# New tokens' scores in a two-layer hybrid decoder step: split products against plain fp32 products

## The chip, the cores and the metric

The kernel runs on one core of one Trainium2 chip. The metric is the device time of one execution in microseconds. Three runs of the kernel before are shown; one more execution was recorded by the hardware profiler, and all rows below come from that one.

## What is computed

Two layers of a decoder run over 1,024 prompt tokens and 64 new tokens (8 sequences of 8). Each layer projects its input to nine parts, mixes one branch with a spatial gMLP (layer norm, a 128x128 product per channel group), mixes the other with three dilated windows of causal attention, gates and merges both, and adds the result. The change touches the scores of the new tokens in window group 0 against the cached keys, and in all three groups against the new keys:

```python
def dilated_gather_attention(q, k_all, v_all, dil, n_back):
    ...
    kg = jnp.take(k_all, idx, axis=1)
    vg = jnp.take(v_all, idx, axis=1)
    s = jnp.einsum('bthd,btjhd->bhtj', q, kg,
                   preferred_element_type=jnp.float32) * (HEAD_DIM ** -0.5)
    s = jnp.where(valid[None, None], s, NEG)
    lse = jax.nn.logsumexp(s, axis=-1)
    p = jnp.exp(s - lse[..., None])
    ...
def att_sample(q, k, v, layer=l):
    ...
    k_all = jnp.concatenate([buf[:, :, 0], k[:, :, g]], axis=1)
```

All data are fp32. Group 0 has 128 cached keys per sequence, all read; the cached keys of groups 1 and 2 are scored elsewhere, on GpSimd and VectorE.

## The kernel before

**The projections set the order.** Per layer 80 jobs (`JOBS`, one job for 128 output columns) are each cut into three pieces of 384, 384 and 320 tokens. A piece (`piece`, L733) is 24 matmuls: weight and activation are each held as a high and a low part in fp32r, and a product is three matmuls (L741). After the third and the sixth of the eight contraction blocks, and behind the piece, `tick` is called. When no attention of the prompt is under way, each tick runs one step of the background queue `bgq` (`bg_step`, L434): first `sample` (L1167), then, in layer 0, `ada` (L555), which prepares the modulation of this layer's end and of the next layer. What a step emits thus stands on TensorE between two thirds of a piece, in an order fixed when the program is written; TensorE runs it in that order and waits where an operand is late.

**The spatial gMLP** (`gmlp`, L1050) sits in a second queue, `urgent`, from the end of the v jobs on. `bg_step` reaches it only when `bgq` is empty; `sample` lets it run where it calls `hurry` (L484), which is also the start of `idle` (L492); `pause` (L488) only gives up steps. The first u job (`ev_u`, L1156) needs it finished: `drain` (L473) then runs the background alone, without pieces between. At the end of a layer another drain (L1603) empties all queues.

**The scores of the new tokens** (`weights` in `sample`, L1204) take two sequences at a time (rg 0 to 3). For each sequence its queries are copied into a block layout `big` and split into high and low parts, twelve small operations on ScalarE and VectorE (L1212, L1213); the new keys are split too (L1214); the cached keys come split from `half_stream` (L315). Then 8 matmuls score the cached keys (L1223) and 24 matmuls of 8 columns the new ones (L1231), and the two halves are added from PSUM (L1236, L1237). Softmax (L1259 to L1263), transposes (L1268) and `outputs` (L1285: value products L1299 to L1311, a reduction on VectorE L1317, a matmul L1321 that waits for it) follow. `units` (L1188) gives the order: scores 0 and 1, outputs 0, scores 2, outputs 1, scores 3, outputs 2 and 3.

Of the kernel before, what the change touches and what calls it, by code (L numbers as in the profile page):

```python
# [32 lines left out]
NB = 8  # L33
# [3 lines left out]
L = 2  # L37
# [142 lines left out]
class Builder:  # L180
# [326 lines left out]
    def setup(self):  # L507
# [28 lines left out]
        self.s_d = [[d([8, NB, NT, 128], f"sd{l}{g}") for g in (1, 2)] for l in range(L)]  # L536
        self.vn_d = [d([3, SMP, 512], f"vnd{l}") for l in range(L)]
# [629 lines left out]
    def sample(self, l):  # L1167
        nc, a, ident = self.nc, self.a, self.pk("ident")
        whole = self.apool.tile([128, 6144], FR, name=self.nm("qb"), tag="act")
        big = whole[:, 0:768]  # L1170
        pt = whole[:, 768:1536].rearrange("p (a b) -> p a b", b=128)
        qs, kn = [whole[:, o:o + 768].bitcast(FT).rearrange("p (a b) -> p a b", b=SMP) for o in (1536, 2304)]
        vw = whole[0:24, 3072:4096].rearrange("p (a b) -> p a b", a=2)
        sel2 = whole[:, 4096:4160]
        knh = whole[:, 4160:4352].rearrange("p (a b c) -> p a b c", a=2, b=12)
        for t, d in ((qs, self.qs_d[l]), (kn, self.kn_d[l])):
            self.load(t, d.rearrange("c p t -> p c t"))
        t = self.half(name="sel2")[:, 0:64]
        self.load(t, a["pack"][:, NPACK:NPACK + 64])
        nc.gpsimd.memset(whole[:, 0:768].bitcast(FT), 0.0)  # L1180
        nc.vector.memset(whole[:, 768:1536].bitcast(FT), 0.0)
        pstep = list(big.ap[0])[0]

        def diag(off, ap, h2):
            v = big[64 * h2:64 * h2 + 64]
            return bass.AP(tensor=v.tensor, offset=v.offset + off, ap=[[pstep, 64]] + ap)
# [3 lines left out]
        for x, rg in units:  # L1190
            for b in (2 * rg, 2 * rg + 1):
                if x == "v":
                    seq += [a["vc1"][l, b, i] for i in range(2)]
                seq.append(a[x + "c0"][l, b])
# [6 lines left out]
        yield from self.idle(2)  # L1201
        pn = {}

        def weights(rg):  # L1204
            rows = self.slot([128, 1024], name="rows")[:, 0:408]
            for b2 in range(2):
                b = 2 * rg + b2
                cols = slice(8 * b, 8 * b + 8)
# [7 lines left out]
                s = [self.ps("s") for _ in range(2)]  # L1216
                hi, lo = next(st)
                for kt in range(4):
                    first, last = kt % 2 == 0, kt % 2 == 1
                    c = slice(kt * 128, kt * 128 + 128)  # L1220
                    mm = [(64, hi), (32, lo)]
                    for m, t in (mm[::-1] if last else mm):
                        nc.tensor.matmul(s[kt // 2][0:m, 0:128], big[:, kt * 64:kt * 64 + m], t[:, c],  # L1223
                                         start=first and m == 64, stop=last and m == 64)
                yield
                for g in range(3):
                    for kt in range(4):
                        base = g * 256 + kt * 64
                        mm = [(64, 0), (32, 1)]
                        for m, e in (mm[::-1] if kt % 2 else mm):  # L1230
                            nc.tensor.matmul(s[kt // 2][0:m, 128 + 8 * g:136 + 8 * g], big[:, base:base + m],  # L1231
                                             knh[:, e, g * 4 + kt, :], start=kt % 2 == 0 and m == 64,
                                             stop=kt % 2 == 1 and m == 64)
                for qd in range(2):
                    t = self.half(name="slo")[0:32, 0:152]
                    self.copy(t, s[qd][32:64, 0:152])  # L1236
                    nc.vector.tensor_tensor(rows[64 * b2 + 32 * qd:64 * b2 + 32 * qd + 32, 128:280], s[qd][0:32, 0:152], t,  # L1237
                                            op=OP.add)
                yield
                yield from self.hurry()  # L1240
# [4 lines left out]
            def scores_in():  # L1245
                for b2 in range(2):
                    for g, o in ((1, 0), (2, 280)):
                        d = self.s_d[l][g - 1]
                        self.load(rows[64 * b2:64 * b2 + 64, o:o + 128],
                                  bass.AP(tensor=d.tensor, offset=d.offset + 1024 * (2 * rg + b2),  # L1250
                                          ap=[[8192, 8], [128, 8], [1, 128]]))
                went.append(True)
# [4 lines left out]
            yield from self.idle(3)  # L1257
# [7 lines left out]
            yield from self.idle(4)  # L1265
# [72 lines left out]

    def q_places(self, qs, pr, cols, h2):
        out = []  # L1340
        for g in range(3):
            src = qs[pr, 4 * g:4 * g + 4, cols].rearrange("p (a b) t -> p a b t", b=2)
            out.append((256 * g + 8 * h2, [[128, 2], [80, 2], [1, 8]], src))
# [361 lines left out]
```

## Time and profile before

| what | value |
|---|---|
| three runs | 3125.6, 3126.67 and 3132.71 us, median 3126.67 us |
| the profiled execution, its time | 3128.81 us |
| its span, first to last instruction | 3127.0 us |
| mean granted TensorE clock | 0.983 of full speed |
| TensorE busy | 3001.5 us, 96% of the span, 19136 matmul records |
| VectorE, GpSimd, ScalarE busy | 54%, 44% and 39% of the span |

In the views below a row of a timeline is one instruction or a merged run of one kind, with its start and duration in us. Matmuls are pipelined, so durations overlap; the time that a group takes is read from its start to the start of the next row. A bracket is the idle time before the row and what ended it. An fp32 matmul leaves two records in the trace, a transpose or an fp32r matmul one.

### The profile page before, as it was taken

How to read it: one execution, taken by the hardware profiler on the slowest of the kernel's cores; microseconds unless marked ns; L12 is line 12 of the kernel's file. 1: busy time of each engine (PE TensorE's matmuls, PEld its weight loads, DVE VectorE, ACT ScalarE, POOL GpSimd, SP SyncE). 2: the span in 40 equal slices, each digit the busy share in tenths (PEclk: the TensorE clock that was granted, in tenths of full speed). 3: DMA queues.
4: the chain of work that ended last, by engine and by line, in shares of the span. 5: the costliest groups of instructions: out<-in, count | busy, mean ns of one | idle time of the engine just before them, and what ended most of it. 6: DMA issues, size and time to landing. Idle time of an engine off the chain costs nothing.

```text
span 3127.0 us, 51203 instructions
## 1 busy us (share of the span) xinstructions
PE 3001.5 (96%) x19136; PEld 2860.7 (91%) x19136; DVE 1702.8 (54%) x3583; ACT 1230.0 (39%) x3085; POOL 1363.7 (44%) x959
## 2 busy tenths in 40 slices
PE   6998999999999999999999989999999999999998
PEld 4998899989999998879989988999999899999998
DVE  7444545463266656466773555464632757553666
ACT  5454444444233133343434544444442331322433
POOL 4665547463144223123446655564731542322343
PEclk8999999999999999999999999999999999999999
DMA  6335243434354334466544253434344542434665
GB/s 223 117 100 113 97 88 119 94 107 95 111 189 142 105 119 163 162 239 228 194 161 130 91 121 99 88 123 85 119 88 128 176 150 89 137 103 144 220 214 178
DMA packets 251537, 425.93 MB, mean 136 GB/s; under 512 B 103852, under 2 KB 158392, under 8 KB 251288
## 3 DMA queue, kind: packets, MB, share of 16 engines
q1 hardware_dynamic: 251288, 422.65, 44.7%
q8 instruction: 151, 2.47, 0.3%
q14 instruction: 98, 0.80, 0.1%
HBM read 349.96 MB, written 72.61 MB: 135 GB/s over the span
## 4 chain that ended last, share of the span: by engine, by line
PE 82%; DVE 7%; DMA 4%; issue 2%; ACT 2%; POOL 1%; SPq 0%; DVEq 0%; ACTq 0%; POOLq 0%
PE pspj L741 53%; PE pspj L1377 13%; PE pss L870 4%; PE pso L916 3%; PE pspt L895 2%; DMA kq<-in_kc_dram 1%; DMA craw<-in_wada_dram 1%; PE psmi L602 1%; DVE chl L249 1%; PE psmi L993 1%; PE pspt L1310 1%; DVE act L249 1%; PE pspt L1127 1%; PE pso L1127 1%; PE pss L1094 1%
## 5 line engine op out<-in xcount | busy, mean ns | idle before, releaser
L741 PE MATMUL pspj<-act,whi 128*128 128x384 f32 (+1 forms) x7680 | 1965.8, 339 | 6.2 <-DVE act L674 3.7
L741 PEld LDWEIGHTS pspj<-act,whi 128*128 128x128 f32 x7680 | 1350.9, 190 | 42.1 <-issue 6.6
L741 PE MATMUL pspj<-act,wlo 128*128 128x384 f32 (+1 forms) x3840 | 1263.0, 329 | 2.3 <-POOL wlo L247 2.3
L249 POOL TENSOR_TENSOR wlo<-wraw,whi 128x1024 fp32r<-128x1024 f32 x154 | 373.2, 2424 | 906.0 <-ACT whi L243 764.4
L741 PEld LDWEIGHTS pspj<-act,wlo 128*128 128x128 f32 x3840 | 728.2, 190 | 3.4 <-POOL wlo L247 3.4
L1377 PE MATMUL pspj<-act,whi 128*128 128x384 f32 (+1 forms) x1536 | 373.5, 326 | 0.5 <-ACT act L243 0.4
L243 ACT ACTIVATE whi<-wraw 128x1024 fp32r<-128x1024 f32 x280 | 294.0, 1052 | 124.3 <-DMA wraw<-in_wgm_dram 49.4
L247 POOL TENSOR_TENSOR wlo<-wraw,whi 128x512 fp32r<-128x512 f32 x126 | 192.2, 1532 | 325.5 <-ACT whi L243 274.7
L882 ACT ACTIVATE ssb<-ssb,ast 128x128 f32<-128x128 f32 (+1 forms) x384 | 170.2, 444 | 380.4 <-DVE ast L878 380.4
L878 DVE CUSTOM_DVE_ANT_0 ssb<-pss,pack 128x128 f32<-128x128 f32 (+1 forms) x384 | 119.4, 348 | 326.7 <-PE pss L870 325.7
L1377 PEld LDWEIGHTS pspj<-act,whi 128*128 128x128 f32 x1536 | 270.2, 188 | 1.0 <-ACT act L243 0.7
L1377 PE MATMUL pspj<-act,wlo 128*128 128x384 f32 (+1 forms) x768 | 250.3, 326 | 0.3 <-POOL wlo L247 0.3
L1005 ACT ACTIVATE th<-pspj 128x384 f32<-128x384 f32 x168 | 79.2, 471 | 422.3 <-PE pspj L741 375.9
L787 POOL TENSOR_TENSOR r<-r,sin 128x384 f32<-128x384 f32 x144 | 139.1, 966 | 175.7 <-DVE r L786 169.9
L249 DVE TENSOR_TENSOR chl<-craw,chl 128x512 fp32r<-128x512 f32 x182 | 155.4, 882 | 86.8 <-ACT chl L243 85.1
L377 POOL TENSOR_TENSOR kq<-kq,qb 128x1024 f32<-128x1024 f32 x64 | 152.6, 2390 | 66.5 <-DMA kq<-in_kc_dram 32.0
L381 POOL TENSOR_TENSOR kq<-kq,qb 128x512 f32<-128x512 f32 x128 | 167.3, 1312 | 30.3 <-DMA kq<-in_kc_dram 25.3
L386 DVE TENSOR_REDUCE sc<-kq 128x16 f32<-128x1024 f32 x128 | 155.7, 1217 | 13.0 <-POOL kq L377 12.9
L870 PE MATMUL pss<-kz,q 128*128 128x256 f32 x560 | 156.2, 387 | 5.6 <-ACT kz L240 5.6
L430 POOL TENSOR_TENSOR vq<-vq,pv 128x1024 f32<-128x1024 f32 x64 | 134.8, 2115 | 49.2 <-DMA vq<-in_vc_dram 25.9
L1377 PEld LDWEIGHTS pspj<-act,wlo 128*128 128x128 f32 x768 | 144.2, 188 | 0.6 <-POOL wlo L247 0.6
L247 DVE TENSOR_TENSOR wlo<-wraw,whi 128x512 fp32r<-128x512 f32 x126 | 108.0, 858 | 43.7 <-ACT whi L243 40.7
(211 smaller groups left out, 3676.6 us busy)
## 6 DMA issues: line engine op xcount, KB each, us to landing
wraw<-in_win_dram SPq DMA_DIRECT2D x160, 512.0 KB
kq<-in_kc_dram SPq DMA_DIRECT2D x64, 512.0 KB
vq<-in_vc_dram SPq DMA_DIRECT2D x64, 512.0 KB
craw<-in_wada_dram SPq DMA_DIRECT2D x48, 512.0 KB
wraw<-in_wgm_dram SPq DMA_DIRECT2D x48, 512.0 KB
wraw<-in_wo_dram SPq DMA_DIRECT2D x48, 512.0 KB
kq<-in_kc_dram SPq DMA_DIRECT2D x64, 256.0 KB
craw<-in_vc_dram SPq DMA_DIRECT2D x32, 512.0 KB
```

The lines of the kernel that those rows point to most:

```text
L243: self.nc.scalar.activation(hi, src, AF.Copy)
L247: e.tensor_tensor(lo[:, c], src[:, c], hi[:, c].bitcast(FT), op=OP.subtract)
L249: (eng or self.nc.vector).tensor_tensor(lo, src, hi.bitcast(FT), op=OP.subtract)
L377: nc.gpsimd.tensor_tensor(v, v, x, op=OP.mult)
L381: nc.gpsimd.tensor_tensor(v[:, f], v[:, 1], x[f], op=OP.mult)
L386: nc.vector.tensor_reduce(sc[:, :, i].rearrange("p h j -> p j h"), ts.pop(i)[0].rearrange("p a (j h d) -> p (a j) h d", h=2, d=64), axis=A ...
L430: nc.gpsimd.tensor_tensor(v, v, p.unsqueeze(3).to_broadcast([128, 2, 8, 64]), op=OP.mult)
L741: nc.tensor.matmul(ps[:, :w], a[:, k, :], h[:, b, k, :w], start=(n == 0), stop=(n == 23))
L787: nc.gpsimd.tensor_tensor(t2, t2, self.sin[:, s], op=OP.mult)
L870: nc.tensor.matmul(s[:, 256 * j:256 * j + 256], u["q"][:, 128 * b:128 * b + 128], self.kz[:, (b - n + j) % 4].rearrange("p h c -> p (h c)" ...
L882: nc.scalar.activation(x[:, h, :w], x[:, h, :w], AF.Exp, bias=st[:, h * 8 + b:h * 8 + b + 1], scale=-1.0, accum_out=st[:, 16 + h * 8 + b:1 ...
L1377: self.nc.tensor.matmul(ps[:, :w], ws[a][:, k, :], hs[b][k][:, :w], start=(n == 0), stop=(n == 3 * nk - 1))
```

## The change

The queries of all sequences are placed once in a block layout `qd` in plain fp32, by DMA into a zeroed tile. All new keys are scored at the start for all sequences in 12 fp32 matmuls of 64 columns (L1209), which give every sequence against every sequence; the result goes through DRAM (`n_d`), and each pair of sequences reads its own 24 columns back. For the cached keys a pair is one batch: its queries are copied into `kz`, the zeroed tile of the prompt's attention, as eight 128x128 blocks, and 8 fp32 matmuls (L1234) add into one PSUM tile. The raw keys are loaded at the start of the pair instead of coming split from the stream. Some `idle` calls become `pause`, and `hurry` stands once at the start of `weights`. The shortened diff:

```diff
+        qd = whole[:, 1536:3072].bitcast(FT).rearrange("p (a b) -> p a b", b=2 * SMP)
...
+        nc.gpsimd.memset(whole[:, 1536:3072].bitcast(FT), 0.0)
+        nc.gpsimd.memset(kz, 0.0)
+        self.load(kn, self.kn_d[l].rearrange("c p t -> p c t"))
+        for h2 in range(2):
+            r = slice(64 * h2, 64 * h2 + 64)
+            self.load(qd[r, :, r], self.qs_d[l][:, r].rearrange("c p t -> p c t"))
...
+        def keys_in(rg):
+            raws[rg] = self.slot([128, 2, 512], name="kraw")
+            for b2 in range(2):
+                self.load(raws[rg][:, b2], a["kc0"][l, 2 * rg + b2])
...
+        t = self.slot([128, 4, 192], name="sn")
+        for g0, n in ((0, 2), (2, 1)):
+            ps = self.ps("s")
+            for c in range(4 * n):
+                nc.tensor.matmul(ps[:, 64 * c:64 * c + 64], qd[:, 4 * g0 + c], kn[:, 4 * g0 + c], start=True, stop=True)
+            for g in range(n):
+                self.copy(t.rearrange("p k (b g t) -> p (k b) g t", b=8, g=3)[:, :, g0 + g],
+                          ps[:, 256 * g:256 * g + 256].rearrange("p (k t) -> p k t", t=8))
+            yield
+        self.store(self.n_d[l].rearrange("k p x -> p k x"), t)
...
         def weights(rg):
+            yield from self.hurry()
             rows = self.slot([128, 1024], name="rows")[:, 0:408]
+            keys_in(rg)
+            for h2 in range(2):
+                v = kz[64 * h2:64 * h2 + 64]
...
+            yield from self.pause(4)
+            k = raws.pop(rg)
+            s = self.ps("s")
             for b2 in range(2):
-                for h2 in range(2):
-                    for o, ap, src in self.q_places(qs, slice(64 * h2, 64 * h2 + 64), cols, h2):
-                        hi, lo = diag(o, ap, h2), diag(o + 32, ap, h2)
-                        self.copy(hi, src)
-                        nc.vector.tensor_tensor(lo, src, hi.bitcast(FT), op=OP.subtract)
-                self.split(knh[:, 0], knh[:, 1], kn[:, :, cols])
-                yield from self.idle(2)
...
                 for kt in range(4):
+                    i = 4 * b2 + kt
+                    nc.tensor.matmul(s[:, 0:128], kz[:, 128 * i:128 * i + 128], k[:, b2, 128 * kt:128 * kt + 128],
+                                     start=i == 0, stop=i == 7)
                 yield
...
-                yield from self.hurry()
+            self.copy(rows[:, 128:256], s[:, 0:128])
...
+                    self.load(rows[64 * b2:64 * b2 + 64, 256:280],
+                              bass.AP(tensor=d.tensor, offset=d.offset + (8 * 192 + 24) * (2 * rg + b2),
+                                      ap=[[12288, 8], [192, 8], [1, 24]]))
...
-            yield from self.idle(3)
+            yield from self.pause(3)
...
-            yield from self.idle(4)
+            yield from self.pause(4)
...
+        nc.gpsimd.memset(kz, 0.0)
```

**Where instructions move.** First TensorE at the first pair of sequences of layer 0. L741 (before) and L742 (changed) are the products of a piece; `pss` is the PSUM tile of the scores. Before, the first part of one sequence:

```order
L741 MATMUL pspj_8672<-act_162,wlo_8585 128x384
L1223 MATMUL pss_8691<-chl_8634,qb_8543 64x128
L1223 MATMUL pss_8691<-chl_8634,qb_8543 32x128 x2
L1223 MATMUL pss_8691<-chl_8634,qb_8543 64x128
L1223 MATMUL pss_8692<-chl_8634,qb_8543 64x128
L1223 MATMUL pss_8692<-chl_8634,qb_8543 32x128 x2
L1223 MATMUL pss_8692<-chl_8634,qb_8543 64x128
L741 MATMUL pspj_8672<-act_162,whi_8584 128x384 x2
```

Now, the first half of the same pair:

```order
L742 MATMUL pspj_8718<-act_165,wlo_8589 128x384
L742 MATMUL pspj_8718<-act_165,whi_8588 128x384 x2
L742 MATMUL pspj_8718<-act_165,wlo_8589 128x384
L1234 MATMUL pss_8746<-kraw_8697,kz 128x128 x4
L742 MATMUL pspj_8751<-act_166,whi_8588 128x320 x2
```

Each sequence had such a group of 8 and, a tick later, one of 24 (L1231); now each has one group of 4, and a layer has 12 matmuls of L1209 once.

The second place is TensorE around the first u job of layer 0, where the gMLP has to be finished (L1127 before and L1128 now are its spatial products, L1094 and L1095 its transposes). Before, its last products stand between two pieces of the job ahead of it, one whole piece before the first u piece:

```order
L741 MATMUL pspj_11351<-act_163,whi_11136 128x384 x2
L741 MATMUL pspj_11351<-act_163,wlo_11137 128x384
L1127 MATMUL pspt_11383<-wm_10727,vn_11361 128x128 x4
L1127 MATMUL pso_11384<-wm_10727,vn_11361 128x128 x4
L741 MATMUL pspj_11401<-act_164,whi_11136 128x320 x2
```

Now, in the drain behind the first piece of the u job:

```order
L742 MATMUL pspj_11103<-act_164,wlo_10959 128x384
L1095 MATMUL pss_11175<-pack,sp_9186 128x128
L1095 MATMUL pss_11175<-pack,sp_9331 128x128
L1095 MATMUL pss_11175<-pack,sp_9475 128x128
L1095 MATMUL pss_11175<-pack,sp_9596 128x128
L1095 MATMUL pss_11176<-pack,sp_9715 128x128
L1095 MATMUL pss_11176<-pack,sp_9854 128x128
L1095 MATMUL pss_11176<-pack,sp_9994 128x128
L1095 MATMUL pss_11176<-pack,sp_10134 128x128
L1128 MATMUL pspt_11192<-wm_10615,vn_11172 128x128 x4
L1128 MATMUL pso_11193<-wm_10615,vn_11172 128x128 x4
L1128 MATMUL pspt_11213<-wm_10615,vn_11210 128x128 x4
```

The whole gMLP begins four pieces later, since scores 3 now run ahead of it; its last stage and the products of the last two stages follow one another there with no piece between, in both layers.

The third place is the end of layer 0, where `ada` (L602 and L579 before, L603 and L580 now) is emptied and the tail's products (L1377, now L1373) begin. Before, at the first of three groups' ends in the drain:

```order
L602 MATMUL psmi_13572<-chl_13616,chl 9x512
L602 MATMUL psmi_13572<-chl_13621,chl 9x512
L602 MATMUL psmi_13572<-chl_13621,chl 18x512
L579 MATMUL psmi_13642<-pack,arow_13640 128x10 x4
L602 MATMUL psmi_13649<-chl_13628,chl 18x512
L602 MATMUL psmi_13649<-chl_13628,chl 9x512
```

Now, at the end of the only group in it:

```order
L603 MATMUL psmi_13319<-chl_13349,chl 9x512
L603 MATMUL psmi_13319<-chl_13354,chl 9x512
L603 MATMUL psmi_13319<-chl_13354,chl 18x512
L580 MATMUL psmi_13365<-pack,arow_13363 128x10 x4
L1373 MATMUL pspj_13379<-ybh_13170,whi_13216 128x384
```

`sample` ends seven pieces earlier, so two more groups of `ada` (16 matmuls and 4 small ones each) find room between pieces.

## Rows read from the trace of the kernel before

**Rows 1.** The page's chain that ended last, shares of the span by engine

```profile
PE 82%; DVE 7%; DMA 4%; issue 2%; ACT 2%; POOL 1%; SPq 0%; DVEq 0%; ACTq 0%; POOLq 0%
```

**Rows 2.** Timeline of PE, scores of one sequence: start, us, instruction, count

```profile
837.93 0.64 PE L1223 MATMUL pss<-chl,qb 128*64 128x128 f32 x8
838.40 0.56 PE L741 MATMUL pspj<-act,whi 128*128 128x384 f32 x2
838.80 0.34 PE L741 MATMUL pspj<-act,wlo 128*128 128x384 f32 x1
838.98 0.51 PE L741 MATMUL pspj<-act,whi 128*128 128x384 f32 x2
839.32 0.33 PE L741 MATMUL pspj<-act,wlo 128*128 128x384 f32 x1
839.49 1.19 PE L1231 MATMUL pss<-qb 128*64 128x8 f32 x24
840.54 0.59 PE L741 MATMUL pspj<-act,whi 128*128 128x384 f32 x2
```

**Rows 3.** Timeline of PE, fp32 products of the gMLP, new tokens, then prompt

```profile
1035.78 1.10 PE L1127 MATMUL pspt<-wsb,vn 64*128 64x64 f32 x8
1036.72 1.05 PE L1127 MATMUL pso<-wsb,vn 64*128 64x64 f32 x8
...
1066.39 1.06 PE L1127 MATMUL pspt<-wm,vn 128*128 128x128 f32 x8
1067.29 1.06 PE L1127 MATMUL pso<-wm,vn 128*128 128x128 f32 x8
```

**Rows 4.** Waits of PE over the span: waited for, us in total, times, longest

```profile
PE pspt L1310 <- DVE chl L249: 7.0, 8, 1.9
...
PE pso L1321 <- DVE oh L1317: 6.2, 4, 2.6
...
PE pss L1223 <- DVE qb L1213: 3.5, 2, 1.7
...
PE pss L1231 <- DVE qb L249: 1.2, 2, 0.6
```

**Rows 5.** Timeline of PE in the drain that ends layer 0, one steady group

```profile
1349.54 1.06 PE L579 MATMUL psmi<-pack,arow 18*128 18x10 f32 x8 [0.73 <-ACT arow L240]
1350.89 3.64 PE L602 MATMUL psmi<-chl,chl 128*18 128x512 f32 x14 [0.29 <-DVE mod L581]
1354.73 0.63 PE L602 MATMUL psmi<-chl,chl 128*9 128x512 f32 x2 [0.20 <-DVE chl L249]
1356.04 1.05 PE L579 MATMUL psmi<-pack,arow 18*128 18x10 f32 x8 [0.68 <-ACT arow L240]
```

**Rows 6.** Timelines of PE, DVE and POOL, the gMLP's last stages in layer 0

```profile
1091.72 1.03 PE L1094 MATMUL pss<-pack,sp 128*128 128x128 f32 x8
1092.59 1.06 PE L1127 MATMUL pspt<-wm,vn 128*128 128x128 f32 x8
...
1098.39 1.04 PE L1094 MATMUL pss<-pack,sp 128*128 128x128 f32 x8
...
1096.07 1.52 DVE L1108 TENSOR_SCALAR vn<-pss,mv 128x512 f32<-128x512 f32 x2
...
1103.85 1.53 DVE L1108 TENSOR_SCALAR vn<-pss,mv 128x512 f32<-128x512 f32 x2 [0.45 <-POOL wlo L249]
...
1101.41 2.40 POOL L249 TENSOR_TENSOR wlo<-wraw,whi 128x1024 fp32r<-128x1024 f32 x1
```

**Rows 7.** Windows around the 2.63 us waits: us, PE, PEld, DVE, ACT, POOL, PEclk, DMA

```profile
1180.00:1190.00 10.00, 7.37 (x38) 7.07 (x38) 9.04 (x18) 3.50 (x11) 2.47 (x2) 0.83 0.54 181
2730.00:2740.00 10.00, 7.37 (x47) 7.07 (x46) 9.13 (x12) 1.28 (x4) 4.40 (x2) 1.00 0.34 109
```

**Rows 8.** Timelines of SP and ACT: one load of cached keys, and its first reader

```profile
840.68 0.38 SPq L252 DMA_DIRECT2D craw<-in_kc_dram  x1
...
845.37 0.62 ACT L243 ACTIVATE chl<-craw 128x512 fp32r<-128x512 f32 x1
```

More of the change, by code (lines that the diff above doesn't have):

```diff
@@ L536, in setup @@
         self.s_d = [[d([8, NB, NT, 128], f"sd{l}{g}") for g in (1, 2)] for l in range(L)]
+        self.n_d = [d([4, 128, 192], f"nd{l}") for l in range(L)]
         self.vn_d = [d([3, SMP, 512], f"vnd{l}") for l in range(L)]
@@ L1169, in sample @@
         whole = self.apool.tile([128, 6144], FR, name=self.nm("qb"), tag="act")
-        big = whole[:, 0:768]
         pt = whole[:, 768:1536].rearrange("p (a b) -> p a b", b=128)
-        qs, kn = [whole[:, o:o + 768].bitcast(FT).rearrange("p (a b) -> p a b", b=SMP) for o in (1536, 2304)]
+        qd = whole[:, 1536:3072].bitcast(FT).rearrange("p (a b) -> p a b", b=2 * SMP)
+        kn = whole[:, 4160:4928].bitcast(FT).rearrange("p (a b) -> p a b", b=SMP)
+        kz = self.kz.rearrange("p a b c -> p (a b c)")
         vw = whole[0:24, 3072:4096].rearrange("p (a b) -> p a b", a=2)
         sel2 = whole[:, 4096:4160]
-        knh = whole[:, 4160:4352].rearrange("p (a b c) -> p a b c", a=2, b=12)
-        for t, d in ((qs, self.qs_d[l]), (kn, self.kn_d[l])):
-            self.load(t, d.rearrange("c p t -> p c t"))
+        nc.gpsimd.memset(whole[:, 1536:3072].bitcast(FT), 0.0)
[4 more added lines that the diff above has]
+            self.load(qd[r, :, r], self.qs_d[l][:, r].rearrange("c p t -> p c t"))
         t = self.half(name="sel2")[:, 0:64]
         self.load(t, a["pack"][:, NPACK:NPACK + 64])
-        nc.gpsimd.memset(whole[:, 0:768].bitcast(FT), 0.0)
         nc.vector.memset(whole[:, 768:1536].bitcast(FT), 0.0)
[L1182 to L1186, printed above, removed]
+        raws = {}
+        def keys_in(rg):
+            raws[rg] = self.slot([128, 2, 512], name="kraw")
+            for b2 in range(2):
+                self.load(raws[rg][:, b2], a["kc0"][l, 2 * rg + b2])
         units = (("k", 0), ("k", 1), ("v", 0), ("k", 2), ("v", 1), ("k", 3), ("v", 2), ("v", 3))
         seq = []
[L1190 to L1194, printed above, removed]
+        for b in range(NB):
+            seq += [a["vc1"][l, b, i] for i in range(2)]
+            seq.append(a["vc0"][l, b])
         st = self.half_stream(seq, 1, 1)
@@ L1202, in sample @@
+        self.store(self.n_d[l].rearrange("k p x -> p k x"), t)
+        del t
         pn = {}
         def weights(rg):
+            yield from self.hurry()
             rows = self.slot([128, 1024], name="rows")[:, 0:408]
-            for b2 in range(2):
-                b = 2 * rg + b2
-                cols = slice(8 * b, 8 * b + 8)
-                for h2 in range(2):
-                    for o, ap, src in self.q_places(qs, slice(64 * h2, 64 * h2 + 64), cols, h2):
-                        hi, lo = diag(o, ap, h2), diag(o + 32, ap, h2)
-                        self.copy(hi, src)
-                        nc.vector.tensor_tensor(lo, src, hi.bitcast(FT), op=OP.subtract)
-                self.split(knh[:, 0], knh[:, 1], kn[:, :, cols])
-                yield from self.idle(2)
-                s = [self.ps("s") for _ in range(2)]
-                hi, lo = next(st)
-                for kt in range(4):
[L1219 to L1224, printed above, removed]
-                yield
[L1226 to L1239, printed above, removed]
-                yield from self.hurry()
@@ new lines, in weights @@
+            keys_in(rg)
+            for h2 in range(2):
+                v = kz[64 * h2:64 * h2 + 64]
+                pstep = list(v.ap[0])[0]
+                self.copy(bass.AP(tensor=v.tensor, offset=v.offset + 8 * h2, ap=[[pstep, 64], [576, 2], [144, 4], [1, 8]]),
+                          qd[64 * h2:64 * h2 + 64, 0:4, 64 * h2 + 16 * rg:64 * h2 + 16 * rg + 16]
+                          .rearrange("p k (b t) -> p b k t", t=8))
+            yield from self.pause(4)
+            k = raws.pop(rg)
@@ L1251, in scores_in @@
                                           ap=[[8192, 8], [128, 8], [1, 128]]))
+                    d = self.n_d[l]
+                    self.load(rows[64 * b2:64 * b2 + 64, 256:280],
+                              bass.AP(tensor=d.tensor, offset=d.offset + (8 * 192 + 24) * (2 * rg + b2),
+                                      ap=[[12288, 8], [192, 8], [1, 24]]))
                 went.append(True)
@@ L1337, in sample @@
         yield
[L1339 to L1343, printed above, removed]
-        return out
     def p_places(self, pt, pn, b2):
```

1 line of the change is left out of this document (added).

## The prediction

> **What bounds the kernel now.** I began with the page's chain of waits: 82% of the span runs over TensorE [rows 1], so time is gained or lost only where TensorE has less or more to do, or where it waits. The second view is TensorE's own timeline. Products follow each other without a gap, and whatever `sample` puts between them pushes the rest back by its whole length: the scores of one sequence are a group of 8 matmuls and one of 24 in the middle of a piece [rows 2]. The third view is the list of what TensorE waits for. The waits tied to `sample` are short and few [rows 4]. The fourth is the clock by windows, since a wait can cost more than its own length [rows 7].
>
> **TensorE's work for the scores.** Removed: per sequence 8 matmuls from 837.93 to 838.40, 0.47 us, and 24 from 839.49 to 840.54, 1.05 us [rows 2]. The two products behind a group take 0.40 us (838.40 to 838.80) where they otherwise take 0.34 (838.98 to 839.32), so each of the two groups costs 0.06 more: 1.64 us per sequence. With 8 sequences in 2 layers that is 16 x 1.64 = 26.2 us.
>
> Added: 64 fp32 products of 128 columns (4 per sequence) and 24 of 64 columns (12 per layer). The nearest rows are fp32 products of the gMLP: 8 records are 4 matmuls, and from one group of 4 to the next it takes 0.90 us with 128 columns and 0.94 us with 64 [rows 3]. The second has 64 contraction rows where the new one has 128, so its price is not shown exactly; between nothing for the missing rows and double, 0.94 to 1.88 for 4, I take 0.94, since the two prices in rows 3 hardly depend on columns or rows. So 16 x 0.90 + 6 x 0.94 = 20.0 us. The balance is **-6.2 us**, at the worst end -0.5.
>
> **Waits that go with it.** TensorE waited 3.5 us for the split queries (L1213) and 1.2 us for the split new keys [rows 4]. Both splits are gone: **-4.7 us**. In their place stand two copies per pair on ScalarE into `kz`, four ticks ahead of the matmuls that read them; I cost them at nothing, covered by the 1.3 pieces between. If that cover went, VectorE and ScalarE being late as they were here, the 4.7 us would stay.
>
> **The raw keys.** They are now loaded at the start of each pair, two loads of 256 KB, and TensorE itself waits for them. No row shows a landing. One such load was read 4.69 us after its issue (840.68 to 845.37) and nothing says that its reader waited [rows 8], so one lands in at most 4.7 us and two in at most 9.4. The four ticks are 32 matmuls apart, at 0.51 us for three (838.98 to 839.49, rows 2) 5.4 us, and SP's queue stands ahead of TensorE by part of a piece, since the only thing it waits for there is the store of a gate of the piece before. Between nothing and 8 x (9.4 - 5.4) = 32 us I take nothing, because that upper end needs two loads one after the other at the longest time. Neither end is a gain.
>
> **Other moves at no cost.** The zeroing of two tiles on GpSimd, which the loads of `qd` wait for on SP, comes several pieces before the first score. Two more small loads per pair (the new keys' scores from DRAM) stand in SP's queue ahead of a weight load, which is wanted a job later, and ahead of the softmax on VectorE; what TensorE takes from the softmax comes four ticks later. The store of `n_d` is waited for by the first of these loads only. VectorE and ScalarE lose a dozen small operations per sequence, but neither bounds here.
>
> **End of layer 0.** Two groups of `ada` leave the drain and go between pieces. Their matmuls cost the same there; what is saved is the waiting between them. In a steady group of the drain TensorE waits 0.29 + 0.20 + 0.68 = 1.2 us [rows 5]. Two groups: **-2.4 us**. The group that stays is still there, with the waits of a beginning.
>
> **The gMLP at the first u job.** This is what the change loses. The gMLP now starts four pieces later, its last stage falls into the drain, and nothing runs between. A stage is the transposes, 0.87 us (1091.72 to 1092.59, rows 6), and the spatial products of the stage before, 0.90 us and a little less, 1.7 together [rows 3]: 2.6 us of TensorE. The normalised rows are ready 5.9 us after its start (1091.72 to 1096.07 + 1.52), or 7.0 us where a weight split of 2.40 us on GpSimd is in the way (1098.39 to 1103.85 + 1.53) [rows 6]. The last stage but one still has 6 matmuls of the piece behind it, 1.0 us; then TensorE needs its PSUM tiles back, and waits 5.9 - 3.6 = 2.3 us (3.4 with the split; 1.5 if the first half frees a tile). The last stage has nothing behind it: 5.9 - 2.6 = 3.3 us (4.4; 2.5). Between 4.0 and 7.8 us I take 5.0 per layer, nearer the lower end, since TensorE can begin when half of the rows are ready: **+10.0 us** for two layers.
>
> **The clock behind it.** Two waits of 2.63 us, of the same kind in the two layers, show both cases: after the one at 1183 the granted clock is 0.83 over 10 us, after the one at 2733 it stays at 1.00 [rows 7]. A clock of 0.83 means a third of the window at 1.2 instead of 2.4 GHz, 3.4 us at half the work: 1.7 us lost. The drain's waits are longer together, so I take a fall in each layer: **+3.4 us**, between 0 and 6.8. By the Trainium skill (page "TensorE: Matmul & The Clock Gate", section "HAM oscillation — how this bites in real kernels") a stall puts the engine back to its lower clock, and the work behind it starts cold. By that rule alone the sum keeps its 3.4 us, by the second window alone it is 3.4 us lower; the first window agrees with the rule, the second does not.
>
> **The sum.** -6.2 - 4.7 - 2.4 + 10.0 + 3.4 = +0.1 us against the profiled execution of 3128.81 us, 2.1 us above the median of the runs. On the median of 3126.67 us the forecast is **3127 us**: no difference that can be measured. A measurement of this kernel tells about 0.3%, 9.4 us, from no change. Between the bounds of the gMLP's waits (8.0 to 15.6) and of the clock (0 to 6.8) the forecast's own range is 3121 to 3136.
>
> **Rivals.**
>
> *Relief on VectorE, faster.* TensorE waits 7.0 us for split values (L1310) and 6.2 us for the reduction in `outputs` (L1321) [rows 4], behind a VectorE that is 9.04 of 10 us busy in the window of the longest [rows 7]. If the lighter load of VectorE takes these waits and the clock's fall at 1183 with them, 7.0 + 6.2 + 1.7 = 14.9 us go: 3112 us. For it: those small operations are on that engine. Against it: the two waits of 2.63 us lie in `outputs` of the last pairs, beside value sums and u jobs that stay, where no score was being split. It decides once two thirds go. Chance 0.14.
>
> *The drain is dearer, slower.* The weight split on GpSimd stands in both stages' way and ahead of the last stage's square root: 7.8 + 2.4 = 10.2 us and a fall of 1.7 per layer are 23.8 us instead of 13.4, and the time is 3137 us. For it: the first u piece starts a job, and the split of the next weights is issued with it, as at 1101.41. Against it: in the stage at 1091 nothing was in the way. It decides from 11.3 us per layer on. Chance 0.09.
>
> *The raw keys land late, slower.* 2 us in each of the eight pairs are 16 us: 3143 us. For it: SP waits for stores of the gates all along here. Against it: the issue stands ahead of the piece in SP's queue. It decides from 1.2 us per pair on. Chance 0.04.
>
> *The products do not get cheaper, slower.* If the new products took double what rows 3 show, 20 us more: 3147 us. Against it: the same form, 128 by 128 by 128 in fp32, is in rows 3. It decides from half as much again. Chance 0.03.
>
> **How the numbers follow.** The forecast has 0.70. Faster by over 0.3% is the first rival, 0.14; slower the other three, 0.16. The range of 3112 to 3138 takes in the forecast's bounds, the full relief and the dear drain, and leaves out the last two rivals and what may lie beyond the first.
>
> **What would show it.** Right: groups of 4 fp32 products at about 0.9 us in place of 0.47 and 1.05; no wait for split queries; at the first u job in each layer two waits of TensorE of 2 to 4 us, at the transposes and at the spatial products, and a clock below 1.00 behind them; one `ada` group in layer 0's last drain instead of three. Wrong: a wait of TensorE for the raw keys; no waits at the first u job; or the waits of `outputs` gone or doubled.

## The result, and the profile after

The changed kernel takes 3157.51 us (median of four runs, 3156.86 to 3158.47) where the kernel before takes 3127.5 us beside it: ratio 1.0077, 95% interval 1.0058 to 1.0096. It is slower by 30 us by the medians, the upper end of that interval, and by 24 us by the ratio; 3127 us was forecast, with 3138 us as the upper end. The profiled execution took 3157.16 us, its span is 3155.4 us, the mean granted clock 0.976.

The chain of waits, as [rows 1]; VectorE and "issue" have gained what TensorE and DMA lost:

```profile
PE 81%; DVE 8%; issue 4%; DMA 3%; ACT 2%; POOL 1%; SPq 0%; DVEq 0%; ACTq 0%; POOLq 0%
```

The new products on TensorE's timeline, as [rows 2], first those of the new keys, then those of one sequence's cached keys:

```profile
835.96 1.00 PE L1209 MATMUL pss<-qb 128*128 128x64 f32 x8
836.77 0.59 PE L742 MATMUL pspj<-act,whi 128*128 128x384 f32 x2
...
843.62 1.05 PE L1234 MATMUL pss<-kraw,kz 128*128 128x128 f32 x8
844.42 0.54 PE L742 MATMUL pspj<-act,whi 128*128 128x320 f32 x2
```

Four products take 0.80 or 0.81 us to the next row, with 64 columns as with 128. They cost what was forecast or a little less.

What TensorE waited for over the span, as [rows 4] (`chl` is a split chunk of cached values, `oh` the result of the reduction, `qb` the split weights of the softmax, `vn` the gMLP's normalised rows):

```profile
PE pspt L1312 <- DVE chl L249: 22.1, 12, 5.7
PE pso L1323 <- DVE oh L1319: 9.8, 6, 3.3
PE pss L1095 <- DVE vn L1109: 7.3, 4, 2.5
PE pspt L1128 <- DVE vn L1109: 4.0, 2, 2.1
...
PE pspt L1301 <- DVE qb L1297: 0.9, 2, 0.6
```

The waits for split queries and split new keys are gone, and none for the raw keys has come. But the value products (L1312) wait 22.1 us for split values where it was 7.0, and the reduction (L1323) 9.8 us where it was 6.2. The list of before has one more row of this kind, at the first value products of a sequence:

```profile
PE pspt L1299 <- DVE qb L1295: 4.4, 3, 2.0
```

So `outputs` waited 7.0 + 6.2 + 4.4 = 17.6 us before and 22.1 + 9.8 + 0.9 = 32.8 us now. The rows of L1095 and L1128, 11.3 us, are the gMLP's last stages.

The longest wait, in outputs 0 (layer 0; layer 1 has 5.09 us at the same place), and the products behind it:

```profile
895.34 0.40 PE L1313 MATMUL pspt<-chl,qb 128*128 128x512 f32 x1
...
902.45 0.69 PE L1312 MATMUL pspt<-chl,qb 128*64 128x512 f32 x1 [5.66 <-DVE chl L249]
902.94 0.63 PE L1313 MATMUL pspt<-chl,qb 128*128 128x512 f32 x1
903.36 0.74 PE L742 MATMUL pspj<-act,whi 128*128 128x320 f32 x2
903.90 0.47 PE L742 MATMUL pspj<-act,wlo 128*128 128x320 f32 x1
...
906.59 0.46 PE L742 MATMUL pspj<-act,whi 128*128 128x320 f32 x2
906.88 0.31 PE L742 MATMUL pspj<-act,wlo 128*128 128x320 f32 x1
```

A pair of products behind the wait takes 0.54 us to the next row (903.36 to 903.90), and 0.29 a few rows later: the clock had fallen. In the kernel before, TensorE came to outputs 0 later and waited less, for the first operand:

```profile
902.70 0.72 PE L1299 MATMUL pspt<-qb 24*128 24x512 f32 x2 [2.04 <-DVE qb L1295]
```

What stood ahead of that chunk, on ScalarE, GpSimd and VectorE:

```profile
892.44 0.63 ACT L243 ACTIVATE qb<-qb 24x512 fp32r<-24x512 f32 x1 [3.15 <-DMA qb<-vnd]
892.98 0.62 ACT L240 ACTIVATE qb<-pn 128x32 fp32r<-128x32 f32 x4
893.51 1.04 ACT L243 ACTIVATE whi<-wraw 128x1024 fp32r<-128x1024 f32 x1
...
897.80 0.63 ACT L243 ACTIVATE acc<-vq 128x512 fp32r<-128x512 f32 x1 [1.44 <-POOL wlo L249]
898.34 0.61 ACT L243 ACTIVATE chl<-craw 128x512 fp32r<-128x512 f32 x1
...
894.70 2.47 POOL L249 TENSOR_TENSOR wlo<-wraw,whi 128x1024 fp32r<-128x1024 f32 x1 [8.46 <-ACT whi L243]
897.13 7.06 POOL L430 TENSOR_TENSOR vq<-vq,pv 128x1024 f32<-128x1024 f32 x3
...
899.98 5.36 DVE L249 TENSOR_TENSOR chl<-craw,chl 128x512 fp32r<-128x512 f32 x3
```

ScalarE stands 3.15 us at new values that are still on their way; the weight split, the value sum (`acc`, from `values`, L401: products on GpSimd at L430, additions on VectorE at L415 and L416) and the chunk are queued behind. Then three splits on VectorE take 5.36 us, beside GpSimd's products, where one takes 0.69 us elsewhere.

The gMLP's last stages in layer 0: one between pieces, and the drain at the first u piece:

```profile
1078.08 1.35 PE L1095 MATMUL pss<-pack,sp 128*128 128x128 f32 x8 [1.15 <-DVE vn L1109]
1079.26 1.06 PE L1128 MATMUL pspt<-wm,vn 128*128 128x128 f32 x8
...
1114.82 0.34 PE L742 MATMUL pspj<-act,wlo 128*128 128x384 f32 x1
1117.66 1.81 PE L1095 MATMUL pss<-pack,sp 128*128 128x128 f32 x8 [2.50 <-DVE vn L1109]
1119.26 1.92 PE L1128 MATMUL pspt<-wm,vn 128*128 128x128 f32 x8
1120.97 1.35 PE L1128 MATMUL pso<-wm,vn 128*128 128x128 f32 x8
1124.26 1.44 PE L1128 MATMUL pspt<-wm,vn 128*128 128x128 f32 x8 [1.94 <-DVE vn L1109]
```

The granted clock in windows, at outputs 0, in the drain, and where the tail of layer 0 begins:

```profile
900.00:910.00 10.00, 7.55 (x35) 7.06 (x36) 6.54 (x6) 1.43 (x5) 4.19 (x2) 0.67 0.44 147
...
1115.00:1125.00 10.00, 5.47 (x31) 4.94 (x31) 7.69 (x19) 1.77 (x2) 2.22 (x2) 0.83 0.17 52
1125.00:1135.00 10.00, 10.00 (x50) 9.02 (x49) 5.10 (x13) 2.31 (x5) 0.00 (x0) 0.83 0.30 100
...
1370.00:1380.00 10.00, 9.32 (x38) 9.13 (x38) 2.17 (x6) 5.37 (x7) 4.21 (x3) 0.66 0.65 256
```

TensorE's clock fell from 2.4 to 1.2 GHz for a third of each of the two windows in the drain, and for longer around the wait at 902 us (0.67); in the kernel before, the windows from 900, 1090 and 1100 us have 1.00. Here the gMLP's own products stand in the fallen clock: transposes take 1.60 us (1117.66 to 1119.26) and not 0.87, spatial products 1.71 and not 0.90. Not all of the first difference is the clock: behind the wait of 1.15 us the transposes take 1.18 us (1078.08 to 1079.26), and the granted clock there is 1.00.

**Where the 30 us are,** from TensorE's rows of both traces over the stretches of `sample` (start to next start, idle time apart): score work 24.8 to 18.0, -6.8; waits for the splits -4.7; end of layer 0 -2.1 (waits 4.9 to 3.9, the matmuls of `ada` 41.1 to 40.0), but the first products of the tail behind it, now at a clock of 0.66, +2.2; waits in the gMLP 2.2 to 11.3, +9.1; its own products +7.1, most of it the lower clock; waits of outputs +15.2; projections and value products at the lower clock behind all these waits some +6. The sum is some +26, of 28 us between the two profiled executions; the rest lies in stretches that the change doesn't touch, and the runs of one kernel spread over more than that. Whether the fall at the tail belongs to the change stays open: of the two traces of the kernel of e1_cadence, one has it and one has not (26.0 and 24.4 us for the same products).

### The profile page after: what moved, and what is told of

The parts are those of the page before. It is cut to its first block, busy times and chain, and to the rows that moved or that the text cites. A ratio compares the mean times of both kernels' runs of the same rounds, so it can differ in the third digit from the quotient of the medians.

```text
span 3155.4 us, 50248 instructions
## 1 busy us (share of the span) xinstructions
PE 3010.3 (95%) x18800; PEld 2870.9 (91%) x18800; DVE 1642.4 (52%) x3423; ACT 1207.7 (38%) x2955; POOL 1368.9 (43%) x963
## 3 DMA queue, kind: packets, MB, share of 16 engines
q8 instruction: 148, 2.42, 0.3%
## 4 chain that ended last, share of the span: by engine, by line
PE 81%; DVE 8%; issue 4%; DMA 3%; ACT 2%; POOL 1%; SPq 0%; DVEq 0%; ACTq 0%; POOLq 0%
PE pspj L742 53%; PE pspj L1373 13%; PE pss L871 4%; PE pso L917 3%; PE pspt L896 2%; DMA kq<-in_kc_dram 1%; PE psmi L603 1%; DVE chl L249 1%; PE psmi L994 1%; DMA craw<-in_wada_dram 1%; DVE act L249 1%; POOL wlo L249 1%; ACT whi L243 1%; PE pspt L1312 1%; DVE vq L416 1%
## 5 line engine op out<-in xcount | busy, mean ns | idle before, releaser
L742 PE MATMUL pspj<-act,whi 128*128 128x384 f32 (+1 forms) x7680 | 1968.9, 339 | 6.1 <-DVE act L675 3.5
L742 PEld LDWEIGHTS pspj<-act,whi 128*128 128x128 f32 x7680 | 1355.7, 191 | 44.8 <-issue 6.6
L742 PE MATMUL pspj<-act,wlo 128*128 128x384 f32 (+1 forms) x3840 | 1265.0, 329 | 1.9 <-POOL wlo L247 1.8
L742 PEld LDWEIGHTS pspj<-act,wlo 128*128 128x128 f32 x3840 | 729.6, 190 | 3.1 <-POOL wlo L247 3.1
L1373 PE MATMUL pspj<-act,whi 128*128 128x384 f32 (+1 forms) x1536 | 373.7, 326 | 0.5 <-ACT act L243 0.4
L1373 PEld LDWEIGHTS pspj<-act,whi 128*128 128x128 f32 x1536 | 270.2, 188 | 1.0 <-ACT act L243 0.7
L1373 PE MATMUL pspj<-act,wlo 128*128 128x384 f32 (+1 forms) x768 | 250.2, 326 | 0.0
L249 DVE TENSOR_TENSOR chl<-craw,chl 128x512 fp32r<-128x512 f32 x166 | 134.3, 839 | 86.4 <-ACT chl L243 85.3
L386 DVE TENSOR_REDUCE sc<-kq 128x16 f32<-128x1024 f32 x128 | 155.7, 1216 | 17.6 <-POOL kq L377 17.1
L430 POOL TENSOR_TENSOR vq<-vq,pv 128x1024 f32<-128x1024 f32 x64 | 135.3, 2125 | 64.9 <-DMA vq<-in_vc_dram 56.9
L1373 PEld LDWEIGHTS pspj<-act,wlo 128*128 128x128 f32 x768 | 144.2, 188 | 0.0
```

Source lines behind the costliest of these rows:

```text
L249: (eng or self.nc.vector).tensor_tensor(lo, src, hi.bitcast(FT), op=OP.subtract)
L386: nc.vector.tensor_reduce(sc[:, :, i].rearrange("p h j -> p j h"), ts.pop(i)[0].rearrange("p a (j h d) -> p (a j) h d", h=2, d=64), axis=A ...
L430: nc.gpsimd.tensor_tensor(v, v, p.unsqueeze(3).to_broadcast([128, 2, 8, 64]), op=OP.mult)
L742: nc.tensor.matmul(ps[:, :w], a[:, k, :], h[:, b, k, :w], start=(n == 0), stop=(n == 23))
L1373: self.nc.tensor.matmul(ps[:, :w], ws[a][:, k, :], hs[b][k][:, :w], start=(n == 0), stop=(n == 3 * nk - 1))
```

## The experiments

Theories A to C were tried first, D to G after their results. All kernels were timed beside the kernel before, whose medians were 3126.4, 3127.1, 3126.0 and 3128.6 us.

**e1_cadence: the old order with the new products.**

```diff
-            yield from self.pause(4)
+            yield from self.idle(6 if rg else 4)
             k = raws.pop(rg)
...
-            yield from self.pause(3)
+            yield from self.idle(3)
...
-            yield from self.pause(4)
+            yield from self.idle(4)
             pp = self.ps("mi")
```

> The changed kernel with the order of the kernel before: every step of sample waits for as many ticks as before, and the steps between let the gMLP run again. TensorE's order is then that of the kernel before, with the new products in place of the split ones. Theory A (the order lost it: outputs that come one piece sooner, and a gMLP that ends at the first u job): the saving of the products is left, 6.8 us of score work and 4.7 us of waits against the kernel before, so about 3116 us; the first wait of outputs is back at the 2.0 us of before, and no wait at the transposes of the gMLP over 1 us. Theory B (the new products, with their zeroed tiles, loads and the way through DRAM, lost it): about 3150 us, near the changed kernel. Theory C (the drain of the gMLP alone, with the waits of outputs as its consequence): about 3116 us as well.

Measured: 3121.16 us, ratio 0.9991 (0.9979 to 1.0003). The loss is gone, so theory B falls: the products, their loads and the zeroing cost nothing that shows. But less is saved than the 11.5 us expected. Its waits:

```profile
PE pso L1323 <- DVE oh L1319: 12.2, 4, 3.4
PE pspt L1312 <- DVE chl L249: 5.4, 8, 0.9
PE pspt L1301 <- DVE qb L1297: 4.1, 2, 2.0
```

Outputs wait 21.7 us, against 17.6 us and 4.7 for the splits before: the 4.7 us came back, most of it at the reduction. The profiled execution of e1_again, the same kernel, has 21.9 us in all, 10.4 of them there.

**e4_v01early: only outputs 0 and 1 early.**

```diff
+            if rg == 3:
+                yield from self.pause(4)
             yield from self.hurry()
...
-            yield from self.pause(4)
+            yield from self.idle(6 if rg == 3 else 4)
             k = raws.pop(rg)
...
```

The two lines behind it are edited as in e1_cadence.

> As e1_cadence, but scores 1 and 2 give up two ticks fewer, so that outputs 0 and 1 come as early as in the changed kernel, while the gMLP runs ahead of scores 3. Theory A: the wait of 5 to 6 us at the value products near 902 us and the one of 2.5 to 3.3 us at the last reduction of outputs 1 stay, about 8 us per layer with the clock behind them, so about 3132 us. Theory B: about 3150 us. Theory C: as e1_cadence, about 3116 us.

Measured: 3135.9 us (1.0032, 1.0018 to 1.0046), 15 us over e1_cadence, with waits of 4.09 and 4.74 us in outputs 0 (2.04 in e1_cadence) and 29.0 us in all outputs. Theory A had 16, theory C none: C falls.

**e6_glate: only the gMLP late.**

```diff
-            yield from self.hurry()
             rows = self.slot([128, 1024], name="rows")[:, 0:408]
...
-            yield from self.pause(4)
+            yield from self.pause(6 if rg in (1, 2) else 4)
             k = raws.pop(rg)
...
-                yield from self.hurry()
+                if rg != 1:
+                    yield from self.hurry()
             del pn[rg]
```

> As e1_cadence for scores 0 to 2 and outputs 0 and 1, but the gMLP runs behind scores 3 as in the changed kernel, one to two pieces later still, and ends in the drain at the first u job. Theory A: the waits of the drain (2.5 and 1.9 us per layer, somewhat more with one more stage in it), a granted clock below 1 there, and the waits of outputs 2 and 3, together about 13 us per layer, less 2 us at the end of layer 0, so about 3140 us; no wait over 2.1 us in outputs 0. Theory B: about 3150 us. Theory C: the time of the changed kernel or more, 3157 us.

Measured: 3157.18 us (1.0107, 1.009 to 1.0123), 36 us over e1_cadence. A said 3140: its drain has one stage more (waits 2.49, 2.31, 2.03 and 1.94 us), and outputs 2 and 3, which come as early on TensorE as in the changed kernel, wait as there. The two effects, 15 and 36, don't add up to the changed kernel's 36 over e1_cadence: here the drain is longer, and the gMLP waits 20.0 us in all where it waits 11.3 in the changed kernel.

**e5_order: the old products in the new order,** an edit of the kernel before.

```diff
         def weights(rg):
+            yield from self.hurry()
...
-                yield from self.idle(2)
+                yield from self.pause((1 if rg else 2) if b2 else (1 if rg else 2))
                 s = [self.ps("s") for _ in range(2)]
...
-                yield from self.hurry()
             while self.scored < 8 * (l + 1):
...
-            yield from self.idle(3)
+            yield from self.pause(3)
...
-            yield from self.idle(4)
+            yield from self.pause(4)
```

> The kernel before, its split products untouched, with the order of the changed kernel alone: fewer ticks in the scores, the gMLP behind scores 3. Theory A: the order costs some 41 us by itself, 30 us of loss and 11 us of saving, so about 3165 us, with the same waits in outputs and in the drain as in the changed kernel. Theory B: the time of the kernel before, 3127 us. Theory C: 3127 us plus the drain alone, about 3145 us or more.

Measured: 3175.32 us (1.0158, 1.0135 to 1.018). The order alone costs 49 us, more than A's 41; the waits for split queries and keys grow too, from 4.7 to 10.4 us. Against it the new products save 18. Theory B is excluded from this side as well.

**f1_tick: one tick more ahead of outputs 2.**

```diff
-                yield from self.idle(3)
+                yield from self.idle(4 if rg == 2 and b2 == 0 else 3)
```

> The changed kernel with one more tick ahead of the value products of outputs 2, and nothing else: the drain of the gMLP stays, outputs 2 and 3 stand on the same ticks of a piece as in e1_cadence. Theory D (the waits of outputs 2 and 3, about 8 us per layer in the changed kernel against 4.6 in e1_cadence, come from the tick on which they stand): the two waits of 1.5 and 1.6 us and the one of 1.3 us at the value products go, one of some 2.9 us at the reduction comes instead of 1.7; about 3 us per layer less, 3151 us. Theory C (they come from the drain just ahead): the waits stay, 3157 us.

Measured: 3148.67 us (1.0067, 1.0053 to 1.0082). The median is 9 us lower, but the intervals overlap, and in layer 0 outputs 2 and 3 wait 6.4 us instead of 7.9: the waits of 1.5 and 1.6 us are replaced by 1.25 and 1.90. The waits move with the tick, so C's reading doesn't hold either, but they don't go where D sent them. It stays undecided.

**f2_splitlate: the split of new values given out two ticks later.**

```diff
+                yield from self.idle(2)
                 self.split(vw[:, 0], vw[:, 1], vraw)
...
-                yield from self.idle(3)
+                yield from self.idle(1)
                 ob = self.ps("pt")
```

> The changed kernel, but in outputs the split of the new values and the copies of the weights are given out two ticks later, still one tick ahead of the products; TensorE's order stays. Theory E (the wait of 5.7 and 5.1 us in outputs 0 comes from ScalarE, which stands 3.2 us at the split of new values that are still on their way, with the weight split, the value sums of GpSimd and the split chunks queued behind it): that stand goes, and the wait falls to about 2 to 3 us; about 3 us per layer less, 3151 us. Rival F (the second chunk of cached values is loaded late, its issue waits 3.7 us on SyncE for a buffer): the wait stays over 5 us, 3157 us.

Measured: 3186.67 us (1.0191, 1.0177 to 1.0205), 29 us worse than the changed kernel. ScalarE no longer stands at the new values (it stands 4.65 us ahead of the value sum's split instead), and the wait for the chunk falls to 0.93 us (2.60 in layer 1), which excludes F. But the operands that are split later are now late themselves:

```profile
898.78 1.22 PE L1302 MATMUL pspt<-qb 24*128 24x512 f32 x2 [3.07 <-DVE qb L1298]
903.89 0.69 PE L1313 MATMUL pspt<-chl,qb 128*64 128x512 f32 x1 [0.93 <-DVE chl L249]
```

E names the queue rightly and its remedy wrongly: over the span 32.6 us are waited for `qb`.

**f3_fin and f4_both: one tick where e1_cadence waits.**

```diff
-                yield
-                yield
+                yield from self.pause(3 if b in (3, 5) else 2)
                 fin = self.ps("o")
```

f4_both has one more:

```diff
-                yield from self.idle(3)
+                yield from self.idle(3 if b else 4)
                 ob = self.ps("pt")
```

> e1_cadence with one more tick between the reduction on VectorE and the matmul that reads it, in sequences 3 and 5 alone, where e1_cadence waits 3.4 and 2.9 us per layer. If TensorE alone sets the pace, both waits go and nothing comes for them: 12 us less than e1_cadence's 3121 us, 3109 us. If outputs are paced by the value sums on GpSimd and VectorE, the wait moves to the next value product: 3118 to 3121 us.

> As f3_fin, and one more tick ahead of the first value products of a layer, where 2.0 us are waited: about 4 us less than f3_fin if that wait goes for good, 3105 us; as f3_fin if it comes back further on.

Measured: 3127.12 us (1.0001, 0.999 to 1.0011) and 3128.12 us (1.0002, 0.9991 to 1.0013): nothing gained, and by the medians some 6 us lost, with intervals that overlap e1_cadence's. The waits of 3.36 and 2.88 us in layer 0 became 2.51 and 1.85, and new ones of 1.17, 1.83 and 2.08 us stand behind them. In all, outputs wait 24.6 and 24.9 us, against 21.7. Time that TensorE gains in outputs is waited for further on.

**g1, g2, g3: without the value sums.**

```diff
             if i % 4:
-                nc.vector.tensor_tensor(ts[i][:, 0], ts[i][:, 0], ts.pop(i - 1)[:, 0], op=OP.add)
-            nc.vector.tensor_tensor(ts[i][:, 0], ts[i][:, 0], ts[i][:, 1], op=OP.add)
+                ts.pop(i - 1)
...
-            nc.gpsimd.tensor_tensor(v, v, p.unsqueeze(3).to_broadcast([128, 2, 8, 64]), op=OP.mult)
             yield
```

> The changed kernel without the value sums of window group 2: the products on GpSimd and the additions on VectorE behind them are left out, the loads, the split of the sums and every step's place stay. Theory G (outputs wait because their splits and reductions stand behind these sums in VectorE's and ScalarE's queues): the waits of outputs, some 16 us per layer with the clock behind them, go nearly all, 3157 - 33 = about 3124 us, and the drain of the gMLP is what is left of the loss. If the waits have to do with the drain or with the loads of the chunks: over 3145 us.

> The kernel before without the same value sums, as the measure for the other two. Theory G: its own waits in outputs and for the split queries, 8 to 10 us per layer, go, 3107 to 3111 us.

> e1_cadence (the new products in the old order) without the value sums. Theory G: the saving of the products is no longer given back to waits in outputs, so it is 7 us of score work and no wait less than g2_before_nosums, about 3100 us, and g1_after_nosums minus this is the drain with its clock less the shorter end of layer 0, 15 to 20 us. If the products save nothing for another reason: as g2_before_nosums.

Measured: 3111.17 us (ratio to the kernel before 0.995), 3095.6 us (0.9897) and 3094.11 us (0.9895). In g1_after_nosums outputs wait 2.5 us in all, where it was 32.8:

```profile
PE pss L1093 <- DVE vn L1107: 7.3, 4, 2.5
PE pspt L1126 <- DVE vn L1107: 4.4, 2, 2.2
PE pspt L1310 <- DVE chl L249: 2.5, 4, 0.7
```

Only the drain is left. So G holds: the changed kernel lies 36 us over e1_cadence with the sums and 17 us without them. 17 us is the drain, with its clock and less the shorter end of layer 0; 19 us is what outputs lose to the sums. Those are medians; over the stretches of `sample` in the traces the changed kernel is 28 us behind e1_cadence with the sums and 14 without, so 14 and 13. The times are 13, 11 to 15 and 6 us lower than G said. The saving of the products, g3 against g2, is 1.5 us by the medians and 3 us over the stretches of `sample` in the traces, or 4.5 without the first products of the tail; the runs of either spread over 4 to 7 us.

**e1_again.**

> e1_cadence once more with more rounds, for the narrower interval: between 3116 and 3122 us, and below the kernel before by 0.1 to 0.3%.

Measured: 3120.73 us, ratio 0.9983 (0.997 to 0.9995). The new products in the old order are faster than the kernel before by 1.6 to 9.4 us in this measurement (the first one's interval reaches no change), and the best of these versions. The traces don't show where: over the stretches of `sample` e1_cadence takes 0.7 us less than the kernel before, and the profiled execution of e1_again, its slowest, 5.5 us more.

**h1_noprod and h2_noadd: half of the sums.**

> The changed kernel without the products of the value sums on GpSimd; the additions on VectorE stay, as many and in the same place. If the additions wait for the products and hold up what stands behind them, or if VectorE's operations are only long beside GpSimd's, nearly all waits of outputs go: 3111 to 3118 us, as in g1_after_nosums. If the additions' own time on VectorE (14 per pair of sequences at 0.7 us) is what the splits and reductions wait for, little changes: over 3140 us.

> The changed kernel without the additions of the value sums on VectorE; the products on GpSimd stay, and the last of each four is what is split. If the additions in VectorE's queue are what holds up the splits behind them, the waits go: 3111 to 3118 us. If the products make ScalarE's split of a sum late, with the split chunks queued behind it there, the wait of 5 us in outputs 0 stays in part, and the time lies between, 3125 to 3145 us.

Measured: 3128.39 us (1.0004, 0.999 to 1.0018) and 3121.76 us (0.9982, 0.9971 to 0.9993). The waits of outputs in h1_noprod:

```profile
PE pso L1322 <- DVE oh L1318: 6.9, 4, 3.2
PE pspt L1311 <- DVE chl L249: 5.5, 10, 0.7
```

In h2_noadd they are 4.2 and 6.9 us. Leaving out either half takes away some 20 of the 32.8 us, and neither takes all. Both times lie between the ranges that were expected, so none of the readings holds in full. Without the products the long wait of outputs 0 is 0.35 us, without the additions 1.92. So both halves are needed for it: the additions in VectorE's queue, and the products. Whether the products matter because the additions wait for them or because they lengthen the operations beside them, these two runs don't tell apart.

## Why the prediction was wrong

- **Score work, -6.2:** right; -6.8 in the rows. The forecast counted the slower products behind a group on the removed side alone; behind a new group they are slower as well (844.42 to 844.80, 0.38 us where 0.29 is usual), and the new groups were cheaper than forecast.
- **Waits for the splits, -4.7:** the waits are gone from the list, but the time isn't. In e1_cadence, where the order is the old one, the waits of outputs are longer by 4.1 us. The step took a wait for a gain without asking what is late next.
- **Raw keys, zeroing, DRAM at nothing:** right; no wait names them, and e1_cadence excludes a cost that shows.
- **End of layer 0, -2.4:** too large. The two groups left the drain, but its waits fell by 1.0 us only, since the group that stays waits 3.9 us where the first of three waited 2.3. With the matmuls of `ada` it is -2.1, and the tail's first products give +2.2 back in the profiled execution.
- **gMLP at the first u job, +10.0:** right in size and place: 2.50 and 1.94 us in layer 0, and 1.15 us at a stage before. Less 2.2 us that the gMLP waited for before, +9.1.
- **The clock, +3.4:** too small. One fall per layer was taken; there are two in the drain. By the forecast's own sum a window of 10 us at 0.83 loses 1.7 us, so four of them lose 6.8 us, its upper bound. The gMLP's own products took 7.1 us longer; part of it is not the clock but the slower start behind a wait (1.18 us for 0.87 at a clock of 1.00), for which the sum had no term. In g1_after_nosums the same waits left one fall per layer (0.83 from 1110 to 1120 us), and these products took 4.4 us longer than in g3_e1_nosums. There the drain with its clock, less the end of layer 0, costs 17 us by the medians and 14 in the traces; the forecast had 10.0 + 3.4 - 2.4 = 11.0. The rule that a stall puts the engine back to its lower clock (the Trainium skill, page "TensorE: Matmul & The Clock Gate", section "HAM oscillation — how this bites in real kernels") is borne out in the drain (0.83 in two windows) and at 902 us (0.67), but not behind every wait: in g1_after_nosums the window from 1100 to 1110 us, with the wait of 2.50 us in it, has 1.00.
- **What failed:** the sum has no term for the place of `outputs`. A pair's scores give up six ticks where they gave up eight. By TensorE's rows outputs 0 come one piece and outputs 1 two pieces sooner in either layer, and outputs 2 and 3 six pieces sooner, behind the drain. The prediction looked at the order at the scores, the u job and the end of the layer, and kept the waits of outputs as they were; its first rival even let them shrink. They nearly doubled, 17.6 to 32.8 us, with some 6 us of clock behind them. What outputs lose against e1_cadence is about 19 us by the medians of the runs with and without the value sums, 13 in the traces. "VectorE and ScalarE lose a dozen small operations per sequence, but neither bounds here" is the sentence that is wrong. In `outputs` VectorE bounds together with GpSimd, through the value sums: without them outputs wait 2.5 us. The text had listed "the waits of `outputs` gone or doubled" as what would make it wrong.
- **The rivals:** the dear drain named the right place, but the waits stayed at 2.50 and 1.94 us, as without a weight split on GpSimd in the way; dearer than forecast is the work behind them. None of them had two causes at once.

What stays open is why single ticks move single waits as they do (f1_tick, f3_fin): the runs show that they do, and that the waits are gone without the sums, but not a rule for the best tick.

## What to carry to other kernels

When a step gives up fewer slots, everything behind it in the program moves, also against queues that keep their own pace: list what comes earlier, and ask whether its operands do. A wait that is removed ahead of a stage that another engine paces was no gain here (e1_cadence, f3_fin); it was waited for at the next operand. Cheaper work and the order that comes with it should be timed apart: here the cheaper products in the old order gain 0.05 to 0.3% in the longer of two measurements, and the new order alone loses 1.6%.

## What was not expected of the hardware

In the changed kernel VectorE's subtraction of two tiles of 128 by 512 takes 0.69 us alone, up to 2.42 us beside a product on GpSimd and up to 2.87 us beside a weight split there; an addition of the same size 0.69, 2.43 and 2.78 us. All 166 splits of chunks of the changed kernel, and then of h1_noprod, where GpSimd's products are left out (columns: busy us, mean ns, idle before):

```profile
L249 DVE TENSOR_TENSOR chl<-craw,chl 128x512 fp32r<-128x512 f32 x166 | 134.3, 839 | 86.4 <-ACT chl L243 85.3 <-PE pspt L1313 0.8
```

```profile
L249 DVE TENSOR_TENSOR chl<-craw,chl 128x512 fp32r<-128x512 f32 x166 | 117.0, 733 | 90.5 <-ACT chl L243 90.3
```

The Trainium skill (page "SBUF — State Buffer", section "Who interferes with whom") says that a VectorE instruction with two inputs in SBUF contends with a GpSimd instruction that reads SBUF, and that the pair of ports that the two share is an exclusive lock. The trace agrees: in the changed kernel 37 of these subtractions and additions take over 0.8 us, and each of them ends 0.55 us after the end of the GpSimd operation that had begun before it, whatever its own length. That is a stop and not a shared speed. One such addition in h1_noprod, where GpSimd's weight splits are still there and the longest is 2.79 us (931.91 + 2.40 = 934.31, 932.07 + 2.79 = 934.86):

```profile
931.91 2.40 POOL L249 TENSOR_TENSOR wlo<-wraw,whi 128x1024 fp32r<-128x1024 f32 x1 [10.89 <-ACT whi L243]
...
932.07 2.79 DVE L415 TENSOR_TENSOR vq<-vq,vq 128x512 f32<-128x512 f32 x1
```

So what a GpSimd operation costs VectorE here is set by when it begins: the three splits ahead of the long wait of outputs 0 took 5.36 us because two of them stood behind products in this way.
